# A decoder layer on one core: low parts moved up in a written order of instructions, and one half sum made by a transfer

## The chip, the cores and the metric

The kernel runs on one core of a Trainium2 chip. The metric is the device time of one launch in microseconds (us). TensorE is PE in the profile, with PEld for its weight loads; VectorE is DVE, ScalarE is ACT, GpSimd is POOL, and SyncE is SP, which issues most of the plain transfers. Accumulating transfers (the target becomes target plus source) are issued by POOL.

## What is computed

One decoder layer on x (512 x 1024, float32). Its second half, where the change lies, is

```python
h = layer_norm(ALPHA * h + mixed @ w_out[l], ln1_g[l], ln1_b[l])
a, u = jnp.split(h @ w_ffn_in[l], 2, axis=-1)      # 1024 -> 2 x 2816
a = causal_dwconv(a, conv_w[l], conv_b[l])
f = (jax.nn.gelu(a, approximate=False) * u) @ w_ffn_out[l]
h = layer_norm(ALPHA * h + f, ln2_g[l], ln2_b[l])
```

The first half (projection, block-sparse attention, mean-pool branch, gates, `w_out`) is not touched.

## The kernel before

**Precision.** Every float32 operand of a large product is cut into a high part, written by ACT as float32r, and a low part, written by DVE as source minus high. PE forms high x high, low x high and high x low, so one block of a product is three matmuls.

**The input product of the channel mixer.** The 2816 columns of a and of u are taken in 22 pairs f of 128 columns each. A pair is a 2 x 2 block product and is done with seven block products instead of eight. Its weight tiles are called A (the raw tile of a), X (128 x 1024, two halves, each a sum of a tile half of u and one of a, made by a plain load and an accumulating load on top of it), D (128 x 512) and Y (128 x 1024, made in the place where A lay). Y's first half is A's first half plus X's second half; Y's second half is A's second half plus Y's first half, so it must come later. The operands on the side of h are h itself (hT) and four sums of its blocks, T3, nT2, T4 and nT1, each with a high and a low part.

**The names of the words.** The block products of pair f are A (24 matmuls), and X0, Y0, D, X1 and Y1 (12 matmuls each). X0 uses T3, Y0 uses nT2, D uses T4 and X1 uses nT1. A 0 or 1 after X or Y says which half of the tile, a number behind an underscore the pair. `fnT13` forms nT1 for the last 128 rows of h (row block 3), `hnT13` writes its high part and `lnT13` its low part; `Thi3` and `Tlo3` write the high and the low part of h itself for row block 3. `hX1` and `lX1` write the high and the low part of the weight tile X of pair 1; `y10` and `y11` make the first and the second half of Y of pair 1 on DVE; `cx`, `cy`, `u1`, `u2` and `s` copy and add partial products between PE's groups.

**What sets the order.** For the end of the first layer norm and the first five pairs, the order on PE, ACT and DVE is written by hand, as one list of words (`line`) of which each calls one step. Each engine runs its own steps in the order of that list. The accumulating transfers on POOL follow a second list, `loads(...)`, called at its place in the program; in it "Y1" stands for one half sum of Y of pair 1, made by an accumulating transfer on chip, and "m3" for a one-element write that holds back the load into that home.

```python
def add_y(key):
    raw = raws[key, "A"]
    n = half_sums.get(key, 0)
    c, o = ((slice(0, S), raws[key, "X"][:, S:]), (slice(S, D), raw[:, :S]))[n]
    POOL.dma_start(raw[:, c], o, accum_op=ALU.add)
    half_sums[key] = n + 1

def form_y(key, c):
    raw = raws[key, "A"]
    o = raw[:, :S] if c else raws[key, "X"][:, S:]
    VEC.tensor_tensor(raw[:, c * S:(c + 1) * S], o, raw[:, c * S:(c + 1) * S], op=ALU.add)
    half_sums[key] = c + 1
```

In the trace nearly all of these instructions carry line 67, the line of the recording helper, so they are told apart by their tiles: `sb<-T_..` is X0 or D of a pair, `saf<-nT_..` is Y0 or X1, `saf<-hT_..` is A or Y1. Both tiles called `own` are homes of A and Y: the first for pair 0, the second for pair 1. X of pairs 1 to 4 lies in `fT`.

Of the kernel before, what the change touches and what calls it, by code (L numbers as in the profile page):

```python
# [73 lines left out]
def layer_kernel(ctx: ExitStack, tc: tile.TileContext, xT, x, w_v, w_c, rel_bias, invcnt, w_group,  # L74
# [124 lines left out]
    def loads(line):  # L199
        POOL.on = True  # L200
        for q, n in line.split():
            key = ("f", int(n))
            if q == "Y":
                add_y(key)
            elif q == "m":
                POOL.memset(x_home(int(n))[:, :1], 0.0)
            else:
                coming[q].remove(key)
                fetch_raw(key, q)
        POOL.on = False  # L210
# [12 lines left out]
    def fetch_raw(key, q):  # L223
        a, u = pair_of[key]
        r = raws[key, q] = homes[key[0], q](key[1])
        if q == "A":
            nc.sync.dma_start(r, a)
        elif q == "D":
            state["D", key] = nc.sync.dma_start(r, u[:, S:])
        elif key in SUMMED:  # L230
            state["plain"] = nc.sync.dma_start(r[:, :S], u[:, :S])
        else:
            v = r.rearrange("p (a c) -> p a c", a=2)
            (pst, pn), (est, _) = u.ap
            state["plain"] = nc.sync.dma_start(
                v, bass.AP(tensor=u.tensor, offset=u.offset, ap=[[pst, pn], [0, 2], [est, S]]))
            state["acc"] = POOL.dma_start(
                v, bass.AP(tensor=a.tensor, offset=a.offset, ap=[[pst, pn], [u.offset + S - a.offset, 2], [est, S]]),
                accum_op=ALU.add)
# [3 lines left out]
# [6 lines that stand above are left out]
# [72 lines left out]
    k1, k2 = slice(0, 4), slice(4, 8)  # L321
# [163 lines left out]
    for kt in range(KT):  # L485
# [3 lines left out]
        last = kt == KT - 1  # L489
# [755 lines left out]
    def x_home(f):  # L1245
        if f in tail or f == 4:
            n = tail[f % 4]
            return fT[:, n:n + 2, :].rearrange("p a c -> p (a c)")
        return xraw[f % 2]
# [4 lines left out]
        return end[0][:, f % 2 * S:(f % 2 + 1) * S]  # L1254

    homes["f", "X"], homes["f", "D"] = x_home, d_home
    loads("X1 m3 D0 X2 m4 D1 D2 X3 D3 X4 D4")

    def first(f):
        n = min(tail.values()) - 1 - f // 2  # L1260
# [92 lines left out]
    for i in (2, 3):  # L1353
        for n in parts:
# [6 lines left out]
              ht3=partial(ln1_T, 3), Traw3=partial(T_raw, 3), Thi3=partial(T_hi, 3), Tlo3=partial(T_lo, 3))  # L1361
# [4 lines left out]
    for f in ahead_:  # L1366
# [17 lines left out]
        })  # L1384
    line = """
        fnT12 fT32 A0 st3 hT32 hnT12 A1 hX0 fnT22 mo lT32 hnT22 inv k0 cl3 A2 hY0 cr3 fT42 rs3 hT42 gl lX0
        ht3 k1 lY0 A3 Traw3 lT42 k2 fnT13 Thi3 lnT22 fT33 A4 lnT12 hT33 fnT23 k3 hD0 lT33 hnT23 fT43 X0_0
        lD0 hT43 lnT23 hX1 lT43 Y0_0 hnT13 y10 cx0 Tlo3 D_0 cy0 lnT13 close last lX1 X1_0 y11 X0_1 s_0 hY1
        u2_0 lY1 Y1_0 cx1 hD1 lD1 Y0_1 hX2 y20 s_2 ga0 D_1 lX2 cy1 u1_0 X1_1 y21 s_3 hY2 s_1 X0_2 u2_1 hD2
        lY2 k4 Y1_1 cx2 u1_1 lD2 Y0_2 hX3 gb0 D_2 cy2 lX3 gg0 y31 X1_2 u1_2 hY3 X0_3 u2_2 ga1 s_4 lY3 hD3  # L1390
        Y1_2 cx3 ge0 lD3 Y0_3 ga2 gb1 hX4 D_3 cy3 lX4 gg1 hY4 X1_3 u1_3 ge1 X0_4 hD4 u2_3 lY4 Y1_3 cx4 lD4
        gb2 Y0_4 hA5 ga3 lA5 D_4 cy4 gg2 gb3 X1_4 ge2 gg3 u2_4 ge3 u1_4
    """.split()
    for word in line:
        do[word]()
# [229 lines left out]
```

## Time and profile before

| | us |
|---|---|
| median of 3 runs | 615.79 (615.68 to 1561.75) |
| the profiled execution, its own time | 615.44 |
| span of the profiled execution | 613.6 |
| PE busy in the span | 606.0 |
| DVE busy | 525.0 |
| ACT busy | 376.5 |
| POOL busy | 140.7 |

The span is what the profiler sees between the first and the last instruction; the execution's own time has 1.84 us more around it. The slices of the page show PE busy in nine tenths or more of every slice but the last.

### The profile page before, as it was taken

The page shows a single profiled execution, that of the slowest core. Times are in us where ns is not written, and L with a number is a line of the kernel's source. Part 1 is how long each engine was busy: PE and PEld are TensorE (multiplying, and loading weights), DVE is VectorE, ACT ScalarE, POOL GpSimd, SP SyncE. Part 2 cuts the span into 40 slices and gives each one's busy share as a digit, 9 for nine tenths or more (in the row PEclk, how much of TensorE's full clock was granted, in tenths as well). Part 3 has the DMA queues.
Part 4 walks back from the last instruction along what each step waited for, and adds up shares of the span by engine and source line. Part 5 has one row for each costly group of instructions (what it writes and reads, how often), then busy time and mean ns, then how long its engine had stood idle before and what let it go on. Part 6 is the DMA issues. An engine that isn't in the chain of part 4 may idle for free.

```text
span 613.6 us, 11150 instructions
## 1 busy us (share of the span) xinstructions
PE 606.0 (99%) x4305; PEld 550.2 (90%) x4305; DVE 525.0 (86%) x807; ACT 376.5 (61%) x580; POOL 140.7 (23%) x161
## 2 busy tenths in 40 slices
PE   9999999999999999999999999999999999999995
PEld 6899998767899998888999999999999998888884
DVE  5978876867878888689999899999999998999985
ACT  6536667657556567337666666666666677655861
POOL 0033207360512101211230110102122132532010
PEclk9999999999999999999999999999999999999998
DMA  8767645147776325955999778686998779999324
GB/s 315 224 189 202 174 135 175 36 120 260 202 189 182 79 84 192 330 134 114 279 176 242 187 188 211 186 204 166 223 251 213 198 166 261 306 206 193 61 48 90
DMA packets 45780, 113.39 MB, mean 185 GB/s; under 512 B 4624, under 2 KB 6552, under 8 KB 45728
## 3 DMA queue, kind: packets, MB, share of 16 engines
q0 software_dynamic: 17856, 42.62, 37.1%
q1 hardware_dynamic: 27440, 69.41, 32.8%
q8 instruction: 34, 0.56, 0.3%
q10 hardware_dynamic: 432, 0.66, 0.3%
q14 instruction: 18, 0.15, 0.1%
HBM read 107.80 MB, written 3.69 MB: 182 GB/s over the span
## 4 chain that ended last, share of the span: by engine, by line
PE 99%; DVE 1%; issue 0%
PE saf L67 25%; PE sbf L67 8%; PE br L67 7%; PE wo L67 7%; PE sag L67 6%; PE foa L67 5%; PE fod L67 5%; PE sai L67 5%; PE sbg L67 3%; PE foe L67 3%; PE v L502 3%; PE fob L67 2%; PE sbi L67 2%; PE sb L67 2%; PE g L67 2%; PE p L67 2%
## 5 line engine op out<-in xcount | busy, mean ns | idle before, releaser
L67 ACT ACTIVATE whi<-araw 128x1024 fp32r<-128x1024 f32 x64 | 67.4, 1059 | 29.7 <-PE saf L67 12.5
L67 DVE TENSOR_TENSOR wlo<-araw,whi 128x1024 fp32r<-128x1024 f32 x62 | 75.9, 1242 | 7.6 <-ACT whi L67 5.7
L67 PE MATMUL saf<-hT_hi,wlo 128*128 128x256 f32 x264 | 73.5, 279 | 0.0
L67 PE MATMUL saf<-hT_hi,whi 128*128 128x256 f32 x264 | 73.5, 278 | 0.0
L67 PE MATMUL saf<-hT_lo,whi 128*128 128x256 f32 x264 | 73.2, 277 | 0.0
L67 POOL DMA_DIRECT2D xraw<-in_w_fi x17 | 20.4, 1201 | 132.3 <-DMA xraw<-in_w_fi 80.8
L67 PEld LDWEIGHTS saf<-hT_hi,whi 128*128 128x128 f32 x264 | 49.6, 188 | 0.1
L67 PEld LDWEIGHTS saf<-hT_lo,whi 128*128 128x128 f32 x264 | 49.5, 188 | 0.1
L67 PEld LDWEIGHTS saf<-hT_hi,wlo 128*128 128x128 f32 x264 | 49.6, 188 | 0.0
L67 PE MATMUL saf<-nT_lo,whi 128*128 128x256 f32 x176 | 49.0, 279 | 0.0
L67 PE MATMUL saf<-nT_hi,whi 128*128 128x256 f32 x176 | 49.0, 279 | 0.0
L67 PE MATMUL saf<-nT_hi,wlo 128*128 128x256 f32 x176 | 48.9, 278 | 0.0
L67 DVE TENSOR_TENSOR wlo<-wraw,whi 128x1024 fp32r<-128x1024 f32 (+1 forms) x31 | 36.3, 1181 | 8.7 <-ACT whi L67 8.5
L67 ACT ACTIVATE whi<-wraw 128x1024 fp32r<-128x1024 f32 (+1 forms) x31 | 31.1, 1013 | 14.9 <-DMA wraw<-in_w_v 4.0
L67 ACT ACTIVATE whi<-xraw 128x1024 fp32r<-128x1024 f32 x25 | 26.5, 1063 | 19.8 <-PE saf L67 12.3
L67 PE MATMUL sbf<-T_hi,whi 128*128 128x256 f32 x136 | 37.8, 278 | 0.0
L67 PE MATMUL sbf<-T_hi,wlo 128*128 128x256 f32 x136 | 37.8, 278 | 0.0
L67 PE MATMUL sbf<-T_lo,whi 128*128 128x256 f32 x136 | 37.7, 277 | 0.0
L67 PEld LDWEIGHTS saf<-nT_lo,whi 128*128 128x128 f32 x176 | 33.0, 188 | 0.3 <-DVE nT_lo L67 0.3
L67 PEld LDWEIGHTS saf<-nT_hi,whi 128*128 128x128 f32 x176 | 33.0, 188 | 0.0
L67 PEld LDWEIGHTS saf<-nT_hi,wlo 128*128 128x128 f32 x176 | 33.0, 188 | 0.0
L67 DVE SCALAR_TENSOR_TENSOR y<-saf,cvp,y 128x511 f32<-128x511 f32 (+1 forms) x44 | 32.7, 744 | 0.1
(455 smaller groups left out, 2099.0 us busy)
## 6 DMA issues: line engine op xcount, KB each, us to landing
araw<-in_w_fi SPq DMA_DIRECT2D x20, 512.0 KB, 4.1
xraw<-in_w_fi SPq DMA_DIRECT2D x17, 512.0 KB, 5.3
xraw<-in_w_fi POOLq DMA_DIRECT2D x17, 512.0 KB, 7.5
araw<-in_w_c SPq DMA_DIRECT2D x12, 512.0 KB, 5.0
tw<-in_w_fo POOLq DMA_DIRECT2D x9, 512.0 KB, 7.8
draw<-in_w_fi SPq DMA_DIRECT2D x17, 256.0 KB, 4.3
wraw<-in_w_br SPq DMA_DIRECT2D x8, 512.0 KB, 4.2
wraw<-in_w_out SPq DMA_DIRECT2D x8, 512.0 KB, 3.8
```

The costliest lines, as they stand in the source:

```text
L67: ins = call(*a, **kw)
L502: ins = nc.tensor.matmul(bs[j], xs_[j][a], (wh, wl)[b], start=kt == 0 and n == 0, stop=False)
```

## The change

Five words of the written order change their place, two words trade places, one word goes, and one word is added to the list of transfers:

- `hnT13` (ACT) goes from behind `Y0_0` to before `A4`.
- `lnT23` (DVE), the low part of nT2, comes ahead of `lD0`, the low part of pair 0's D tile.
- `lnT13` (DVE), the low part of nT1, comes ahead of `Tlo3`, the low part of h; the calls `close` and `last` (release of a pool, later transfers) go with it.
- `y10` (DVE) goes. The same sum is made by an accumulating transfer, "Y1" in the list of transfers behind "D2".
- `s_0` and `u2_0` (both DVE) trade places.
- `hY4` and `hD4` (ACT) trade places with words of other engines, which leaves the order on each engine as it is.

```diff
-    loads("X1 m3 D0 X2 m4 D1 D2 X3 D3 X4 D4")
+    loads("X1 m3 D0 X2 m4 D1 D2 Y1 X3 D3 X4 D4")
...
-        ht3 k1 lY0 A3 Traw3 lT42 k2 fnT13 Thi3 lnT22 fT33 A4 lnT12 hT33 fnT23 k3 hD0 lT33 hnT23 fT43 X0_0
-        lD0 hT43 lnT23 hX1 lT43 Y0_0 hnT13 y10 cx0 Tlo3 D_0 cy0 lnT13 close last lX1 X1_0 y11 X0_1 s_0 hY1
-        u2_0 lY1 Y1_0 cx1 hD1 lD1 Y0_1 hX2 y20 s_2 ga0 D_1 lX2 cy1 u1_0 X1_1 y21 s_3 hY2 s_1 X0_2 u2_1 hD2
...
+        ht3 k1 lY0 A3 Traw3 lT42 k2 fnT13 Thi3 lnT22 fT33 hnT13 A4 lnT12 hT33 fnT23 k3 hD0 lT33 hnT23 fT43
+        X0_0 lnT23 hT43 lD0 hX1 lT43 Y0_0 cx0 lnT13 close last Tlo3 D_0 cy0 lX1 X1_0 y11 X0_1 u2_0 hY1 s_0
+        lY1 Y1_0 cx1 hD1 lD1 Y0_1 hX2 y20 s_2 ga0 D_1 lX2 cy1 u1_0 X1_1 y21 s_3 hY2 s_1 X0_2 u2_1 hD2 lY2 k4
```

On DVE, from the low part of T3 to the low part of pair 1's Y tile (`own<-fT,own` is `y10`, `own<-own` is `y11`, `saf<-fT,saf` is `s_0`, `fT<-fT,saf` is `u2_0`), it stood so before:

```order
L67 TENSOR_TENSOR wlo_3504<-fT,whi_3503 128x512
L67 TENSOR_TENSOR nT_lo<-hraw,nT_hi 128x4x128
L67 TENSOR_TENSOR T_lo<-hraw,T_hi 128x4x128
L67 TENSOR_TENSOR own_2889<-fT,own_2889 128x512
L67 TENSOR_TENSOR hT_lo<-ht_0_3420,hT_hi 128x8x64
L67 TENSOR_TENSOR hT_lo<-ht_1_3421,hT_hi 128x8x64
L67 TENSOR_TENSOR nT_lo<-hraw,nT_hi 128x4x128
L67 TENSOR_TENSOR wlo_3526<-fT,whi_3525 128x1024
L67 TENSOR_TENSOR own_2889<-own_2889 128x512
L67 TENSOR_TENSOR saf_3313<-fT,saf_3313 128x256
L67 TENSOR_TENSOR fT<-fT,saf_3313 128x256
L67 TENSOR_TENSOR wlo_3606<-own_2889,whi_3605 128x1024
```

The same place on DVE stands so now:

```order
L67 TENSOR_TENSOR nT_lo<-hraw,nT_hi 128x4x128
L67 TENSOR_TENSOR wlo_3506<-fT,whi_3505 128x512
L67 TENSOR_TENSOR T_lo<-hraw,T_hi 128x4x128
L67 TENSOR_TENSOR nT_lo<-hraw,nT_hi 128x4x128
L67 TENSOR_TENSOR hT_lo<-ht_0_3421,hT_hi 128x8x64
L67 TENSOR_TENSOR hT_lo<-ht_1_3422,hT_hi 128x8x64
L67 TENSOR_TENSOR wlo_3528<-fT,whi_3527 128x1024
L67 TENSOR_TENSOR own_2889<-own_2889 128x512
L67 TENSOR_TENSOR fT<-fT,saf_3314 128x256
L67 TENSOR_TENSOR saf_3314<-fT,saf_3314 128x256
L67 TENSOR_TENSOR wlo_3606<-own_2889,whi_3605 128x1024
```

Both low parts of the h sums have moved one place or three places up, `y10` is gone, and `y11` (`own<-own`) is one place nearer.

On POOL, where the transfers for X of pairs 1 to 4 (`fT<-in_w_fi`) are issued, it stood so before:

```order
L67 DMA fT<-in_w_fi 128x2x512
L67 MEMSET fT 128x1
L67 DMA fT<-in_w_fi 128x2x512
L67 MEMSET fT 128x1
L67 DMA fT<-in_w_fi 128x2x512 x2
L67 DMA araw_3048<-fT 128x512
```

The same place on POOL stands so now:

```order
L67 DMA fT<-in_w_fi 128x2x512
L67 MEMSET fT 128x1
L67 DMA fT<-in_w_fi 128x2x512
L67 MEMSET fT 128x1
L67 DMA own_2889<-fT 128x512
L67 DMA fT<-in_w_fi 128x2x512 x2
L67 DMA araw_3048<-fT 128x512
```

The new half sum (`own<-fT`) is issued behind X's accumulating loads of pairs 1 and 2 and ahead of those of pairs 3 and 4.

## Rows read from the trace of the kernel before

**Rows 1.** The page, part 1: PE's busy time and share of the span.

```profile
PE 606.0 (99%) x4305; PEld 550.2 (90%) x4305; DVE 525.0 (86%) x807; ACT 376.5 (61%) x580; POOL 140.7 (23%) x161
```

**Rows 2.** PEld's waits over the span: us in total, times, longest.

```profile
PEld saf L67 <- DVE nT_lo L67: 0.3, 2, 0.2
...
PEld foa L67 <- ACT whi L67: 0.4, 1, 0.4
```

**Rows 3.** The chain, 293 to 335 us: start, length, what.

```profile
301.56 1.63 PE saf L67 x12
303.19 1.39 PE sb L67 x12
304.57 1.61 PE saf L67 x12
...
307.57 2.77 PE saf L67 x24
```

**Rows 4.** DVE in order of time, 278 to 345 us: start, length, what.

```profile
300.29 0.69 DVE L67 TENSOR_TENSOR wlo<-fT,whi 128x512 fp32r<-128x512 f32 x1
300.89 0.69 DVE L67 TENSOR_TENSOR nT_lo<-hraw,nT_hi 128x512 fp32r<-128x512 f32 x1
...
302.10 0.69 DVE L67 TENSOR_TENSOR own<-fT,own 128x512 f32<-128x512 f32 x1
...
303.90 0.69 DVE L67 TENSOR_TENSOR nT_lo<-hraw,nT_hi 128x512 fp32r<-128x512 f32 x1
...
305.63 0.69 DVE L67 TENSOR_TENSOR own<-own 128x512 f32<-128x512 f32 x1
...
307.45 1.23 DVE L67 TENSOR_TENSOR wlo<-own,whi 128x1024 fp32r<-128x1024 f32 x1 [0.26 <-ACT whi L67]
```

**Rows 5.** ACT in order of time, 278 to 345 us.

```profile
298.06 0.63 ACT L67 ACTIVATE T_hi<-hraw 128x512 fp32r<-128x512 f32 x1 [1.27 <-DVE hraw L67]
...
306.36 1.06 ACT L67 ACTIVATE whi<-own 128x1024 fp32r<-128x1024 f32 x1 [2.75 <-DVE own L67]
```

**Rows 6.** POOL in order of time, 270 to 365 us: its issues of transfers.

```profile
291.19 1.20 POOL L67 DMA_DIRECT2D fT<-in_w_fi  x1 [4.42 <-DMA fT<-in_w_fi]
...
297.05 1.19 POOL L67 DMA_DIRECT2D fT<-in_w_fi  x1 [4.55 <-DMA fT<-in_w_fi]
...
...
307.35 1.20 POOL L67 DMA_DIRECT2D fT<-in_w_fi  x1 [1.09 <-DMA fT<-in_w_fi]
311.74 0.89 POOL L67 DMA_DIRECT2D araw<-fT  x1 [3.19 <-DMA fT<-in_w_fi]
```

**Rows 7.** DMA issues, 291 to 291.5 us: KB, us from issue to landing.

```profile
fT<-in_w_fi POOLq DMA_DIRECT2D x1, 512.0 KB, 9.2
```

**Rows 8.** DMA issues, 297 to 297.2 us.

```profile
fT<-in_w_fi POOLq DMA_DIRECT2D x1, 512.0 KB, 8.9
```

**Rows 9.** DMA issues, 307.3 to 307.6 us.

```profile
fT<-in_w_fi POOLq DMA_DIRECT2D x1, 512.0 KB, 6.9
```

**Rows 10.** DMA issues, 311.7 to 311.8 us.

```profile
araw<-fT POOLq DMA_DIRECT2D x1, 256.0 KB, 3.9
```

**Rows 11.** DMA issues over the span: the on-chip half sums of pairs 0 and 4.

```profile
own<-y POOLq DMA_DIRECT2D x1, 256.0 KB, 3.3
...
araw<-araw POOLq DMA_DIRECT2D x1, 256.0 KB, 6.3
```

**Rows 12.** DMA queues, 301 to 305 us: packets, MB, share of 16 engines.

```profile
q0 software_dynamic: 253, 0.50, 66.9%
```

**Rows 13.** DMA queues, 305 to 307 us.

```profile
q1 hardware_dynamic: 185, 0.33, 48.8%
q0 software_dynamic: 15, 0.02, 6.5%
```

**Rows 14.** Busy time by stretch (PE, PEld, DVE, ACT, POOL), then PE's clock, DMA.

```profile
606.00:608.00 2.00, 0.20 (x1) 0.00 (x0) 1.86 (x8) 0.62 (x2) 0.46 (x1) 1.00 0.65 61
...
609.00:610.00 1.00, 0.00 (x0) 0.00 (x0) 0.96 (x3) 0.24 (x1) 0.00 (x0) 0.50 1.13 225
```

More of the change, by code (lines that the diff above doesn't have):

```diff
@@ L1386, in layer_kernel @@
         fnT12 fT32 A0 st3 hT32 hnT12 A1 hX0 fnT22 mo lT32 hnT22 inv k0 cl3 A2 hY0 cr3 fT42 rs3 hT42 gl lX0
-        ht3 k1 lY0 A3 Traw3 lT42 k2 fnT13 Thi3 lnT22 fT33 A4 lnT12 hT33 fnT23 k3 hD0 lT33 hnT23 fT43 X0_0
-        lD0 hT43 lnT23 hX1 lT43 Y0_0 hnT13 y10 cx0 Tlo3 D_0 cy0 lnT13 close last lX1 X1_0 y11 X0_1 s_0 hY1
-        u2_0 lY1 Y1_0 cx1 hD1 lD1 Y0_1 hX2 y20 s_2 ga0 D_1 lX2 cy1 u1_0 X1_1 y21 s_3 hY2 s_1 X0_2 u2_1 hD2
-        lY2 k4 Y1_1 cx2 u1_1 lD2 Y0_2 hX3 gb0 D_2 cy2 lX3 gg0 y31 X1_2 u1_2 hY3 X0_3 u2_2 ga1 s_4 lY3 hD3
-        Y1_2 cx3 ge0 lD3 Y0_3 ga2 gb1 hX4 D_3 cy3 lX4 gg1 hY4 X1_3 u1_3 ge1 X0_4 hD4 u2_3 lY4 Y1_3 cx4 lD4
-        gb2 Y0_4 hA5 ga3 lA5 D_4 cy4 gg2 gb3 X1_4 ge2 gg3 u2_4 ge3 u1_4
+        ht3 k1 lY0 A3 Traw3 lT42 k2 fnT13 Thi3 lnT22 fT33 hnT13 A4 lnT12 hT33 fnT23 k3 hD0 lT33 hnT23 fT43
+        X0_0 lnT23 hT43 lD0 hX1 lT43 Y0_0 cx0 lnT13 close last Tlo3 D_0 cy0 lX1 X1_0 y11 X0_1 u2_0 hY1 s_0
+        lY1 Y1_0 cx1 hD1 lD1 Y0_1 hX2 y20 s_2 ga0 D_1 lX2 cy1 u1_0 X1_1 y21 s_3 hY2 s_1 X0_2 u2_1 hD2 lY2 k4
+        Y1_1 cx2 u1_1 lD2 Y0_2 hX3 gb0 D_2 cy2 lX3 gg0 y31 X1_2 u1_2 hY3 X0_3 u2_2 ga1 s_4 lY3 hD3 Y1_2 cx3
+        ge0 lD3 Y0_3 ga2 gb1 hX4 D_3 cy3 lX4 gg1 X1_3 u1_3 hY4 ge1 X0_4 u2_3 hD4 lY4 Y1_3 cx4 lD4 gb2 Y0_4
+        hA5 ga3 lA5 D_4 cy4 gg2 gb3 X1_4 ge2 gg3 u2_4 ge3 u1_4
     """.split()
```

## The prediction

> **What bounds the kernel.** I read the page first: PE is busy for 606.0 of 613.6 us [rows 1], so an edit moves the time only where PE waits, or where it makes PE wait. The list of PEld's waits over the span is next. Of the many entries only one names a step that this change moves: the low part of an nT sum, twice, 0.3 us together [rows 2]. The chain in order of time gives the price. A group of 12 matmuls takes 1.39 us. The two groups that hold these waits, `Y0_0` at 301.56 and `X1_0` at 304.57, take 1.63 and 1.61 us [rows 3], so they lose 0.24 and 0.22 us, together 0.46. This is a little more than the waits themselves, and it is all that the moved words can win.
>
> **Who is late.** DVE in order of time answers that. `lnT23` ends at 300.89 + 0.69 = 301.58, just as `Y0_0` begins; `lnT13` ends at 303.90 + 0.69 = 304.59, just as `X1_0` begins [rows 3, 4]. Ahead of them stand `lD0` (300.29), `y10` (302.10) and the low part of h. DVE's starts in this stretch lie 0.60 us apart for such instructions (300.29, 300.89), though each is listed with 0.69 [rows 4].
>
> **The moved words, part by part.** `lnT23` takes `lD0`'s place and ends at 300.29 + 0.69 = 300.98; its high part stood ahead of it before as well. PE's group wants it 0.6 us later, so the 0.24 us go. `lD0` then ends at 301.58; the group that reads it, `D_0`, starts at 303.19 - 0.24 = 302.95, so this costs nothing, with 1.4 us of cover. `lnT13` takes `y10`'s place and ends at 302.10 + 0.69 = 302.79; `X1_0` starts at 304.57 - 0.24 = 304.33, so the 0.22 us go. This needs `hnT13` earlier on ACT, where it now stands before the instruction that sat idle for 1.27 us until 298.06 [rows 5]. Such an instruction takes 0.63 us, so it fits; without that idle time it would push the high part of T3 by 0.63 us. The low part of h keeps its place in time: one instruction of DVE comes ahead of it where another goes. `u2_0` and `s_0` trade places between PE's groups and cost nothing by themselves. Sum of the moves: -0.46 us.
>
> **The half sum as a transfer.** `y10` took 0.60 us of DVE's queue, so DVE reaches `y11` at 305.63 - 0.60 = 305.03. But `y11` reads what the transfer writes, and now waits for it to land. When is that? The transfer reads X of pair 1, whose accumulating load was issued at 291.19 and landed 9.2 us later, at 300.39 [rows 6, 7]. So it is not issued before 300.4. It goes behind the load for X of pair 2, issued at 297.05 and landed 8.9 us later, at 305.95 [rows 6, 8]. The trace of before has no transfer in this place, so I bound its landing:
> - From below, as if nothing stood ahead of it: the half sums of pair 0 took 3.3 us from issue to landing [rows 11], which gives 303.7. That of pair 4, in a busier stretch, took 6.3 [rows 11], which gives 306.7.
> - As POOL's queue behaves further on: X of pair 4 was issued at 307.35 and landed at 314.25; the half sum of pair 3, issued at 311.74 while that load was on its way, landed at 315.64, 1.39 us behind it [rows 6, 9, 10]. The same here gives 305.95 + 1.39 = 307.34.
> - From above, at the pace of the stretch itself: 512 KB took POOL's queue 305.95 - 300.39 = 5.56 us, so 256 KB take 2.78, which gives 308.73.
>
> I take 307.34. The queues decide that for me: between 301 and 305 us POOL's queue, q0, moved 0.50 MB, just the 512 KB of pair 2's load, which had been issued at 297.05 and so lay still until pair 1's had landed [rows 8, 12]. From 305 to 307 q0 moved almost nothing [rows 13]. So the new 256 KB find their place in that gap and not ahead of it.
>
> [...]
>
> **What stands behind the wait.** On DVE `y11`, `u2_0`, `s_0` and `lY1` are queued in this order, and ACT's `hY1` needs `y11`. Before, `lY1` ended at 307.45 + 1.23 = 308.68, which is 3.05 us after `y11` began; ACT's `hY1`, 1.06 us, is the middle of that path [rows 4, 5]. With the transfer at 307.34 the path ends at 310.39. Who wants it: PE's `Y0_1`. The 2.77 us from 307.57 are `Y1_0` and `Y0_1` [rows 3], so `Y0_1` began at 308.96, and with the 0.46 us won it would begin at 308.50. Its third matmul reads the low part, two twelfths of a group (0.23 us) later, at 308.73. So PE waits 310.39 - 308.73 = 1.66 us. Part of that is met one group earlier: `Y1_0` may not begin until `u2_0` has read its bank, and `u2_0` stands behind `y11`; the two waits lie in one another and are not added. For the restarts and the step from a landing to the waiting engine I add 0.2 us, an estimate from rows 2 and 3, where two waits of 0.3 us together cost 0.46. Sum: +1.86 us.
>
> **Does it come back later?** PE stays the bound from here to the end, so a lag of PE is kept. The one later wait in the list, for a high part of an output weight (0.4 us), is priced as it was [rows 2]. X of pairs 3 and 4 queues behind the new 256 KB, which lie in the gap of q0 up to 307, so I cost that at nothing; without the gap their landing moves by 1.4 us, on tiles that PE reads later than all of the above.
>
> **Net and the time.** -0.46 + 1.86 = +1.40 us on the profiled execution's 615.44, so 616.84. The median of the runs lies 0.35 us above that execution (615.79), so the forecast is **617.2 us**. Worked from the bounds of the landing: the loss is zero up to about 305.5 and grows by 1 us for each us beyond; 305.9 is the break-even against the 0.46 won. At 306.7 the net is +0.8 (616.6), at 308.73 it is +2.8 (618.6).
>
> **Rival 1: the transfer lands in time, the kernel is faster.** If the transfer is moved beside pair 2's load instead of behind it, it lands between 303.7 and 305.5, `y11` finds its data and only the 0.46 us won remain: 615.79 - 0.46 = 615.3. For it: the 3.3 us of pair 0's half sums, and the half sum of pair 3 took only 3.9 us from its issue although a load was on its way [rows 10, 11]. Against: pair 2's load itself lay still for 3 us in this very stretch. It decides for this rival if the landing is before 305.5.
>
> **Rival 2: the two waits are won, and the transfer is only a little late.** A landing between 305.5 and 306.7 gives a net between -0.46 and +0.8, so 615.3 to 616.6. The 6.3 us of pair 4's half sum are the row for its upper end.
>
> **Rival 3: PE's wait drops its clock, the kernel is slower by more.** [...] Against it: the forecast wait is in two pieces with a full group between them, and is shorter than the one in rows 14.
>
> **Rival 4: the waits are not won.** Another low or high part could be late in place of the nT sums, for which `hnT13` on ACT and `lD0` are the candidates. Both have cover (0.6 and 1.4 us), so I give it little. With the transfer in time it makes 615.8, no change.
>
> **How the numbers follow.** Chances: forecast (landing beyond 306.7) 0.60, rival 1 0.21, rival 2 0.12, rival 3 0.03, rival 4 0.04. The likeliest gives 617.2, with 616.6 to 618.6 as its own range. The range for 8 in 10 has to reach down to rival 1, so it runs from 615.2 to 618.4, which leaves out rival 3 and the last part of the upper bound. All but the far end of rival 3 lie within 2% (12.3 us), about what a measurement of this kernel can tell from no change: within 2% 0.98, slower 0.01, faster 0.01.
>
> **What the profile of the changed kernel would show.** The groups at 301.56 and 304.3 take 1.39 us each, and the nT entry is gone from PEld's waits: this shows the moves right. DVE sits idle for about 2.3 us before `own<-own`, put down to the transfer `own<-fT`, which takes nearly 7 us from issue to landing; PE waits for DVE near 307 and again near 310; and q0 is busy between 305 and 307 us. If instead `own<-fT` lands within 5 us of its issue and DVE doesn't idle, rival 1 holds. The prediction would be wrong by its queueing step, then, and by nothing else of weight.

## The result and the profile after

The changed kernel takes **619.49 us** (median of 6 runs, 617.47 to 620.64) against 615.73 of the kernel before on the same chip: a ratio of 1.006, 95% interval 1.0041 to 1.0079. That is 3.76 us slower, where the forecast was 1.40 us slower and its range ended at 618.4. The profiled execution of the changed kernel took 620.32 us, with a span of 618.6 us.

The page, part 1, of the changed kernel: PE's busy time and share.

```profile
PE 607.6 (98%) x4305; PEld 551.8 (89%) x4305; DVE 524.5 (85%) x806; ACT 376.3 (61%) x580; POOL 141.8 (23%) x162
```

As many matmuls as in [rows 1], 1.6 us more busy, in a span that is 5.0 us longer. So most of the loss is PE idle, and a part of it is PE busy for longer with the same work.

PE's and PEld's waits in the changed kernel over its span: us in total, times, longest.

```profile
PE saf L67 <- DVE saf L67: 2.3, 1, 2.3
...
PE foa L67 <- ACT whi L67: 0.6, 1, 0.6
...
PEld saf L67 <- DVE saf L67: 2.5, 1, 2.5
```

The entry for nT_lo of [rows 2] is gone, so the two waits that the moved words aimed at are won. A wait of 2.3 us has come in their place. (The longer wait for an output weight, `foa`, belongs to this one execution: another execution of the same kernel, below, doesn't have it.)

PE of the changed kernel in order of time: the first matmuls of `Y0_0`, `D_0`, `X1_0` and `X0_1`, and the last one before the wait.

```profile
301.78 0.28 PE L67 MATMUL saf<-nT_hi,whi 128*128 128x256 f32 x1
...
303.17 0.28 PE L67 MATMUL sb<-T_hi,whi 128*128 128x256 f32 x1
...
304.55 0.28 PE L67 MATMUL saf<-nT_hi,whi 128*128 128x256 f32 x1
...
305.94 0.28 PE L67 MATMUL sb<-T_hi,whi 128*128 128x256 f32 x1
...
307.21 0.28 PE L67 MATMUL sb<-T_hi,wlo 128*128 128x256 f32 x1
```

`Y0_0` and `X1_0` now take 303.17 - 301.78 = 1.39 and 305.94 - 304.55 = 1.39 us.

The chain of the changed kernel from 301 us on, which now leads from transfers through DVE to PE: start, length, what.

```profile
301.24 6.98 DMA own<-fT
...
308.25 0.04 DVE own L67
308.29 0.57 issue
308.86 0.42 DVE fT L67
...
309.31 0.44 DVE saf L67
...
309.79 4.48 PE saf L67 x24
314.27 1.39 PE sb L67 x12
```

In [rows 3] the same stretch was PE alone. Read it downwards: the half sum is issued at 301.24, when X of pair 1 has landed, it lands 6.98 us later, DVE does `y11`, `u2_0` and `s_0` (0.04 + 0.57, 0.42, 0.44 us), and only then does `Y1_0` begin. The row of 24 matmuls is the second loss: `Y1_0` and `Y0_1` together took 2.77 us in [rows 3] and take 4.48 here.

DVE of the changed kernel in order of time, to be held against [rows 4].

```profile
300.67 0.69 DVE L67 TENSOR_TENSOR nT_lo<-hraw,nT_hi 128x512 fp32r<-128x512 f32 x1
...
302.48 0.69 DVE L67 TENSOR_TENSOR nT_lo<-hraw,nT_hi 128x512 fp32r<-128x512 f32 x1
...
308.25 0.69 DVE L67 TENSOR_TENSOR own<-own 128x512 f32<-128x512 f32 x1 [2.75 <-DMA own<-fT]
```

Both nT low parts are earlier, as forecast, and DVE idles for 2.75 us before `y11` and is released by the transfer.

POOL of the changed kernel in order of time: its issues, to be held against [rows 6].

```profile
297.32 1.19 POOL L67 DMA_DIRECT2D fT<-in_w_fi  x1 [4.36 <-DMA fT<-in_w_fi]
...
301.24 0.89 POOL L67 DMA_DIRECT2D own<-fT  x1 [2.62 <-DMA fT<-in_w_fi]
```

DMA issues of the changed kernel, 297.2 to 297.5 us: KB, us to landing.

```profile
fT<-in_w_fi POOLq DMA_DIRECT2D x1, 512.0 KB, 9.0
```

DMA queues of the changed kernel, 305 to 307 us: packets, MB, share.

```profile
q0 software_dynamic: 154, 0.28, 76.1%
```

Pair 2's load lands at 297.32 + 9.0 = 306.32, just as late after its issue as in [rows 8], and the half sum at 301.24 + 6.98 = 308.22, 1.9 us behind it. POOL's queue, almost idle between 305 and 307 us in [rows 13], is now filled there.

The stretches of the changed kernel: busy time of PE, PEld, DVE, ACT and POOL, then PE's granted clock, the DMA share and GB/s.

```profile
307.00:308.00 1.00, 0.49 (x5) 0.29 (x3) 0.00 (x0) 0.00 (x0) 0.00 (x0) 1.00 0.90 227
308.00:309.00 1.00, 0.00 (x0) 0.00 (x0) 0.75 (x2) 0.03 (x1) 0.07 (x1) 1.00 0.96 178
309.00:310.00 1.00, 0.21 (x1) 0.21 (x2) 0.70 (x2) 1.00 (x2) 1.00 (x1) 0.74 1.10 205
310.00:311.00 1.00, 1.00 (x5) 1.00 (x6) 0.94 (x1) 1.00 (x4) 0.13 (x1) 0.50 1.14 148
311.00:312.00 1.00, 1.00 (x7) 1.00 (x6) 1.00 (x3) 0.77 (x1) 0.00 (x0) 0.50 0.48 78
312.00:313.00 1.00, 1.00 (x7) 1.00 (x6) 1.00 (x3) 0.24 (x1) 0.28 (x1) 0.55 1.09 201
313.00:314.00 1.00, 1.00 (x11) 1.00 (x11) 1.00 (x2) 0.54 (x1) 0.72 (x2) 1.00 1.10 203
```

Here is the rest of the loss. PE stops in the second half of 307 us and is idle until 309.79; the granted clock falls from 1.00 to 0.50 and stays there until shortly before 313 (0.50 from 312.50 to 312.75, 0.72 on average from 312.75 to 313.00). It fell before PE was at work again: from 309 to 310 us PE worked only the last 0.21 us, and the mean clock of that microsecond is already down to 0.74; from 309.40 to 309.60 it is 0.69, from 309.60 to 309.79 it is 0.50, both with PE idle. In the three microseconds from 310 to 313 PE is listed as fully busy and yet issues 5 to 7 matmuls per microsecond instead of 11.

### The profile page after: what moved, and what is told of

Its sections match the earlier page's. It is cut to its first block, busy times and chain, and to the rows that moved or that the text cites. A ratio compares the mean times of both kernels' runs of the same rounds, so it can differ in the third digit from the quotient of the medians.

```text
span 618.6 us, 11153 instructions
## 1 busy us (share of the span) xinstructions
PE 607.6 (98%) x4305; PEld 551.8 (89%) x4305; DVE 524.5 (85%) x806; ACT 376.3 (61%) x580; POOL 141.8 (23%) x162
## 4 chain that ended last, share of the span: by engine, by line
PE 93%; DMA 5%; DVE 1%; issue 0%; ACT 0%; SPq 0%; ACTq 0%
PE saf L67 22%; PE sbf L67 8%; PE br L67 7%; PE wo L67 7%; PE sag L67 6%; PE fod L67 5%; PE sai L67 5%; PE foa L67 4%; PE sbg L67 3%; PE foe L67 3%; PE v L502 3%; PE fob L67 2%; DMA fT<-in_w_fi 2%; PE sbi L67 2%; PE g L67 2%; PE p L67 2%
```

## The experiments

Diffs are against the changed kernel, unless said otherwise. The theory is: the moves win 0.46 us; the transfer queues behind pair 2's load and holds up `Y1_0`; the idle PE then loses its clock.

**The two halves of the change apart.** In moves_only the half sum is back on DVE.

```diff
-    loads("X1 m3 D0 X2 m4 D1 D2 Y1 X3 D3 X4 D4")
+    loads("X1 m3 D0 X2 m4 D1 D2 X3 D3 X4 D4")
-  ... Y0_0 cx0 lnT13 close last Tlo3 ...
+  ... Y0_0 cx0 lnT13 y10 close last Tlo3 ...
```

> The changed order, but the first half of pair 1's Y sum is again made by VectorE, behind nT1's low part, and the transfer is gone. Theory (the whole loss is the wait for the transfer and what follows from it; the moved low parts win 0.46 us): 0.46 us under the kernel before, about 615.3, with the two groups of Y0_0 and X1_0 at 1.39 us each. Rival (the moves themselves, or the swap of the two small steps behind them, cost something): at or above 615.8, or above it by 1 us and more.

Measured: 615.48 against 615.33 us, ratio 0.9998 (0.9989 to 1.0007), no change. The interval reaches as far down as 0.46 us, so the time alone can't tell this gain from none. The chain of moves_only, start, length, what, shows where most of it went:

```profile
302.03 1.39 PE saf L67 x12
303.41 1.39 PE sb L67 x12
304.80 1.39 PE saf L67 x12
306.19 1.50 PE sb L67 x12
307.69 3.01 PE saf L67 x24
```

`Y0_0` and `X1_0` are down to 1.39 us, but the groups behind them grew by 0.11 and 0.24 us, so 0.35 of the 0.46 us is given back. With `y10` behind `lnT13`, DVE hands over `y11` and what follows later. The moves alone shift the lateness from one step to the next; it takes one instruction less on DVE for them to pay, as sum_on_gpsimd shows below.

In transfer_only the order is that of before, without `y10` and with the transfer (diff against the kernel before).

```diff
-    loads("X1 m3 D0 X2 m4 D1 D2 X3 D3 X4 D4")
+    loads("X1 m3 D0 X2 m4 D1 D2 Y1 X3 D3 X4 D4")
-  ... Y0_0 hnT13 y10 cx0 Tlo3 ...
+  ... Y0_0 hnT13 cx0 Tlo3 ...
```

> The order before, with the one VectorE sum replaced by the transfer, at the same place in the list of transfers as in the change. Theory: the transfer lands at the same time, so PE stalls as in the changed kernel and its clock falls; the 0.46 us are not won, and freeing 0.6 us on VectorE wins nothing: 619 to 620.5. Rival (the loss needs the swapped steps or the earlier release of the pool): below 617.

Measured: 617.85 against 615.33 us, ratio 1.0042 (1.0028 to 1.0056). PE's wait in transfer_only and, after it, two stretches of that kernel:

```profile
PE saf L67 <- DVE fT L67: 2.2, 1, 2.2
```

```profile
309.00:310.00 1.00, 0.35 (x3) 0.35 (x4) 0.64 (x3) 1.00 (x3) 0.92 (x1) 1.00 1.15 213
310.00:311.00 1.00, 1.00 (x11) 1.00 (x10) 1.00 (x2) 1.00 (x3) 0.00 (x0) 1.00 0.72 100
```

The transfer alone makes the wait and, without any of the moves, a slowdown of 2.5 us. This is less than the 619 to 620.5 us expected, since the clock held at 1.00 in this profile. By the mean granted clock of each execution (0.997 to 0.998 in four, 0.994 in one, which took 619.57 us against 617.27 to 617.96) it held in four of five.

**Is it the order in the queue?** Two kernels move the transfer in POOL's list: ahead of pair 2's load, and behind pair 3's.

```diff
-    loads("X1 m3 D0 X2 m4 D1 D2 Y1 X3 D3 X4 D4")
+    loads("X1 m3 D0 Y1 X2 m4 D1 D2 X3 D3 X4 D4")    transfer_first
+    loads("X1 m3 D0 X2 m4 D1 D2 X3 Y1 D3 X4 D4")    transfer_later
```

> The changed kernel, with the half sum issued ahead of the accumulating load for X of pair 2 instead of behind it. Theory (the transfer is late because it queues behind that load): it lands 3.3 to 5 us after its issue at about 301, so between 304.3 and 306, PE waits for at most 1 us and the clock holds: 615.3 to 616.5. Pair 2's load, issued some 4 us later than before, lands near 309 and is read at about 308.4, so up to 1 us of wait may come in its place. Rival (the transfer is slow by itself in this busy stretch, in whatever place): it takes near 7 us again and the time stays at 619 or more.

Measured: 617.92 against 615.33 us, ratio 1.0046 (1.0033 to 1.0059). The DMA issue of transfer_first, KB and us to landing:

```profile
own<-fT POOLq DMA_DIRECT2D x1, 256.0 KB, 3.4
```

With nothing ahead of it the transfer lands 3.4 us after its issue, not 7.0: what it waits for in the changed kernel is pair 2's load. The time is lost elsewhere, since POOL issues pair 2's load only at 301.92 us and it lands at 310.12. PE then waits 0.6 us until 312.20 for a copy by ACT, which stands on ACT behind the high part of that late tile, and further on 0.8 us until 331.93 for a low part of DVE and 0.4 us until 335.60 for another copy by ACT. The clock stays at 1.00. So the change of place moved the loss from one tile to later ones.

> The changed kernel with the half sum issued one place later still, behind the accumulating load for X of pair 3. Theory (the transfer lands behind whatever load stands ahead of it in POOL's queue): that load landed at 311.5 to 312.5 in every run so far, so the half sum lands at about 313 to 314, some 5 us later than in the changed kernel; PE's wait grows to 7 us or more, the clock falls in every execution, and the time is 623 to 626. Rival (the landing is set by the busy stretch before 307 and not by the load ahead): it lands near 309, as in the changed kernel, and the time stays at 619 to 621.

Measured: 624.36 against 615.18 us, ratio 1.0144 (1.0131 to 1.0158), so 9.2 us slower. The chain of transfer_later and, after it, its stretches:

```profile
306.18 6.43 DMA own<-fT
...
314.17 5.49 PE saf L67 x24
```

```profile
312.00:313.00 1.00, 0.00 (x0) 0.00 (x0) 0.37 (x1) 0.00 (x0) 0.93 (x2) 0.89 1.10 201
313.00:314.00 1.00, 0.00 (x0) 0.00 (x0) 0.97 (x3) 0.64 (x1) 0.00 (x0) 0.50 1.13 209
```

One place further back in the queue, the landing moves to 312.61 and PE's wait grows to 6.7 us. The clock is again down before PE starts, and it stays down under all 24 matmuls (0.50 from 314 to 315, 0.54 on average from 315 to 320), which take 5.49 us instead of 2.77. The stall of 6.7 and the 2.7 us of clock, less 0.46, make 8.9 of the 9.2 us.

**Is it the clock?** If PE is given other work while it waits, the wait shrinks and the clock should hold. One, two or three groups of 12 matmuls are put ahead of `Y1_0`; their product is used by nothing.

```diff
+    do["fill"] = lambda: s_mm(("f", 1), "X", 0, tt["T3"], low_(2), True)
-        lY1 Y1_0 cx1 ...
+        lY1 fill Y1_0 cx1 ...               one_group
+        lY1 fill fill Y1_0 cx1 ...          filled_wait
+        lY1 fill fill fill Y1_0 cx1 ...     three_groups
```

> The changed kernel with two extra groups of 12 matmuls (a repeat of pair 1's X0 group, into the bank that pair 2 overwrites later) put where PE waits; 2.77 us of added PE work whose result isn't used. Theory (the wait costs twice, once as a stall of about 2.4 us and once as the lower clock behind it, about 1.6 us): the stall is filled, the clock stays at 1.00, and the kernel with the added work is faster than the changed one, by about 1.5 us: 618.0. Rival (the slow matmuls behind the wait come from something else, such as the transfers): they stay slow, and the time is that of the changed kernel or up to 0.4 us more.

Measured: 618.20 against 615.33 us, ratio 1.0043 (1.0031 to 1.0056). The chain of filled_wait:

```profile
301.45 8.32 DMA own<-fT
...
311.33 3.05 PE saf L67 x24
```

The clock held in every execution (mean 0.996 to 0.998) and the 24 matmuls take 3.05 us. PE still waits 0.9 us, as the transfer landed later here (8.3 us from its issue). With 2.77 us of useless work added, the median lies below that of the changed kernel, though their intervals overlap.

> The changed kernel with one extra group of 12 matmuls (1.39 us of PE work whose result isn't used) where PE waits. Theory: 1 us of the wait is left, the clock holds, and the time is that of an execution of the changed kernel whose clock held, about 617.4 to 618. Rival (any wait of this place lowers the clock): 619 and more.

Measured: 619.07 against 615.55 us, ratio 1.0051 (1.0036 to 1.0066). Two stretches of one_group:

```profile
311.00:312.00 1.00, 1.00 (x10) 1.00 (x10) 1.00 (x1) 1.00 (x3) 0.00 (x0) 0.92 0.89 152
312.00:313.00 1.00, 1.00 (x7) 1.00 (x6) 1.00 (x3) 0.94 (x2) 0.62 (x2) 0.50 1.12 207
```

The transfer landed 8.3 us after its issue here as well, so that the wait was 2.3 us as before, in spite of the added group, and the clock fell, here only when PE had been at work again since 310.71. By the mean clock it fell in two of the six executions (0.995, 619.73 and 619.99 us) and held in four (0.997 to 0.998), of which three took 618.53 to 619.18 us all the same. The run does not separate the theories: it changed the work and, by chance or not, the landing with it.

> The changed kernel with three extra groups of 12 matmuls (4.16 us of PE work whose result isn't used) where PE waits. Theory: they cover the wait even where the transfer lands 8.3 us after its issue, so no wait and no lower clock is left: the kernel before, minus 0.46, plus 4.16, so 3.7 us above it, in every execution, with a mean clock of 0.996 or more; the changed kernel, which has none of this work, takes 3.8 to 4.3 us more than the kernel before. Rival (other costs of the transfer remain): 5 us and more above the kernel before.

Measured: 618.83 against 615.18 us, ratio 1.006 (1.0047 to 1.0073), 3.65 us more. The chain of three_groups, where one row holds `X0_1` and the three added groups:

```profile
305.69 5.55 PE sb L67 x48
311.24 2.77 PE saf L67 x24
```

No wait is left, the clock stays at 1.00, and the 24 matmuls take 2.77 us again. The added work, 3 x 1.39 = 4.16 us, less the 0.46 won, is 3.70 us: as expected. The changed kernel, which has none of that work, is as slow. So its stall and its clock together cost about as much as 36 matmuls, and no further cost of the transfer shows.

**The changed kernel once more,** unaltered, since its six runs spread over 3 us.

> The changed kernel itself, beside the next three on one chip. Theory (a stall of about 2.4 us, and in most executions a lower clock behind it for 1.6 us): two kinds of executions, near 617.4 with a mean granted clock of 0.997 or more and near 619.4 with 0.995 or less, more of the second kind. Rival (the spread is in the transfer's landing and not in the clock): the times spread evenly and don't go with the clock.

Measured: 619.88 against 615.55 us, ratio 1.0069 (1.0052 to 1.0086). The profiled execution was by chance the fastest, 617.72 us. Its stretches and, after them, its chain:

```profile
309.00:310.00 1.00, 0.57 (x4) 0.57 (x5) 0.67 (x2) 1.00 (x3) 0.77 (x1) 1.00 1.10 203
310.00:311.00 1.00, 1.00 (x11) 1.00 (x10) 1.00 (x2) 1.00 (x2) 0.00 (x0) 1.00 1.03 98
```

```profile
309.43 3.06 PE saf L67 x24
```

The same program, the same wait (2.4 us), a held clock: 3.06 us for the 24 matmuls against 4.48, and no wait for `foa`. This is the cleanest price of the clock, 4.48 - 3.06 = **1.42 us**. The other five executions, with a mean clock of 0.992 to 0.995, took 619.55 to 621.65 us. In the first series it was alike: 617.47 us at a mean clock of 0.997, the other five 619.22 to 620.64 at 0.993 to 0.995. In these ten the fall is read from the mean clock (0.996 and more in every execution of the kernel before) and the time; only two executions have a trace, one that lost its clock and one that kept it. The transfer landed 7.0 and 7.1 us after its issue in these two and up to 8.5 in other runs, so a later landing may have added to the time of some of the ten.

**Can the wait be covered by order alone?** In y11_behind `u2_0` and `s_0` go ahead of the waiting `y11`, so that `Y1_0` isn't blocked by them.

```diff
-  ... X1_0 y11 X0_1 u2_0 hY1 s_0 lY1 Y1_0 cx1 ...
+  ... X1_0 X0_1 u2_0 s_0 y11 Y1_0 hY1 lY1 cx1 ...
```

> The changed kernel with the waiting VectorE step (the second half of pair 1's Y sum) put behind the two small steps that PE's next group needs. Theory: the transfer lands as before, PE goes on for one group more and then waits in two pieces, for the high and the low part of that tile, about 2.2 us in all; no wait is as long as the 2.3 us in the changed kernel, so the clock holds in every execution: about 617.3, some 2 us under the changed kernel. Rival (the length of PE's wait in one piece doesn't matter for the clock): as the changed kernel, 619 and more.

Measured: 620.36 against 615.55 us, ratio 1.008 (1.0068 to 1.0092). It was expected to do better and didn't. `Y1_0` does run without a wait. PE then stops one group later, 2.7 us for ACT's high part and 0.7 us for DVE's low part, as the transfer landed 8.5 us after its issue, and the clock is down to 0.50 by 314 us. By the mean clock it fell in three of the five executions (0.993); the two others (0.996) took as long, 620.17 and 620.36 us, so here the clock doesn't tell the times apart. `Y0_1` needs the sum itself, and no order on DVE changes when that lands.

**The same sum without a queue.** In sum_on_gpsimd the changed order stays, and GpSimd makes the half sum by an instruction at the place where it issued the transfer. gpsimd_only is transfer_only with the same edit.

```diff
-    POOL.dma_start(raw[:, c], o, accum_op=ALU.add)
+    if key == ("f", 1):
+        POOL.tensor_tensor(raw[:, c], o, raw[:, c], op=ALU.add)
+    else:
+        POOL.dma_start(raw[:, c], o, accum_op=ALU.add)
```

> The changed order, with the first half of pair 1's Y sum made by a GpSimd instruction at the place where the transfer stood in its queue. Theory (the moved low parts win 0.46 us if VectorE is freed of 0.6 us and nothing waits for the queue of transfers): the sum takes about 1.7 us, as the GpSimd sums of the same size earlier in the kernel, starts when X of pair 1 has landed, near 301, and ends near 303, two us before it is read; 0.3 to 0.5 us faster than the kernel before. Rival (GpSimd is slower beside a busy VectorE, or slows it): no gain, or a wait of PE as in the changed kernel.

Measured: 614.50 against 615.55 us, ratio 0.9986 (0.9978 to 0.9994). POOL and, after it, the chain in sum_on_gpsimd:

```profile
301.28 3.18 POOL L67 TENSOR_TENSOR own<-fT,own 128x512 f32<-128x512 f32 x1 [2.63 <-DMA fT<-in_w_fi]
```

```profile
302.10 1.39 PE saf L67 x12
...
304.87 1.39 PE saf L67 x12
...
307.64 2.77 PE saf L67 x24
```

The sum is there at 301.28 + 3.18 = 304.46, before DVE reaches `y11`, every group takes its 1.39 us, and PE doesn't wait between 290 and 330 us. The instruction is longer than the 1.7 us expected (one GpSimd sum of that shape took 1.68 us, at 240.40 in the kernel before); POOL had nothing else to do.

> The order before, with the one VectorE sum made by a GpSimd instruction, at the place in GpSimd's queue where the change had the transfer. Theory: VectorE is 0.6 us ahead from that place on, so the wait of X1_0 (0.22 us) goes and that of Y0_0 (0.24 us) stays: 0.2 us under the kernel before, about half of what the changed order with the same GpSimd sum won. Rival (the GpSimd sum alone makes the gain, or none of it): as far under the kernel before as with the changed order, or not under it.

Measured: 615.26 against 615.18 us, ratio 0.9995 (0.9986 to 1.0004), not to be told from no change. The chain of gpsimd_only:

```profile
301.43 1.63 PE saf L67 x12
```

`Y0_0` still takes 1.63 us there, as in [rows 3], so the moves are needed for its 0.24 us.

> The changed order with the half sum as a GpSimd instruction, a second time on another occasion, since its first result (ratio 0.9986, 0.9978 to 0.9994) lies close to no change. Theory: the two waits that the moved words win (0.46 us) are won and nothing is lost, so about 0.5 us below the kernel before (ratio 0.9993), and the first result's 1.05 us were in part scatter. Rival: the gain of about 1 us is real, ratio near 0.9985, and something beyond the two waits is won. Third: no gain, ratio 1.000. In the profile every group of 12 between 300 and 315 us takes 1.39 us and the clock stays at 1.00.

Measured: 615.39 against 615.52 us, ratio 0.9997 (0.9988 to 1.0006), with every group at 1.39 us again. So of the two series one is just below the kernel before and one is level with it. The profile shows both waits won, 0.46 us. The times fit that, and don't measure it: 1.05 us in the first series is more than the trace accounts for, 0.13 in the second is less. As the better way to write this change it is clear of the scatter: 4 to 5 us below the changed kernel.

## Why the prediction was off

**Right.** The moved words win 0.46 us: the two groups went from 1.63 and 1.61 [rows 3] to 1.39 us, and `Y1_0` would have begun 0.46 us earlier on a common clock (PE's first matmul of `X0_0` starts 0.38 us later in the profile after). That they win only if DVE is relieved as well was not said; moves_only shows it. The direction, the place, DVE's idle time before `y11`, the 7 us of the transfer and the filled q0 came as forecast, and transfer_first and transfer_later show the step from the queue's order. Rivals 1 and 2, an early landing, fall, and so does rival 4, since the two waits are won.

**Off in size: the stall.** Three sums, of the profile after:
- Landing. Forecast 1.39 us behind pair 2's load, from the half sum of pair 3 [rows 9, 10]; measured 308.22 - 306.32 = 1.90. That is 0.5 us more.
- The path behind it. The forecast followed the long way over `lY1` to `Y0_1` and said that the wait comes in two pieces. It came in one, at `Y1_0`: `s_0` had been put behind `u2_0`, both stand behind `y11`, and from the landing to PE's start it is 309.79 - 308.22 = 1.57 us. The long path ends later, but PE has all of `Y1_0` to do before it needs it; the short one ends first, and PE has nothing to do until then. So the short one decides. PE's last matmul before it started at 307.21, so `Y1_0` was due 0.12 us later, at 307.33, and lost 2.46 us.
- Restart: in changed_again, at full clock, the first 0.12 us go there.

Together 2.58 us where the forecast had 1.86.

**The step that failed: that the clock holds.** The forecast has no term for the clock and leaves its fall to rival 3, which was given a chance of 0.03, because the wait would be "in two pieces with a full group between them, and is shorter than the one in rows 14". The first half of that was wrong, as shown. The second was no argument: in the stretch of [rows 14] one wait of 1.9 us (606.20 to 608.12) ended at clock 1.00, and the clock was down about one microsecond later (0.81 on average from 608.80 to 609.00, 0.50 from there on); that doesn't show a wait that is safe. In ten of twelve executions of the changed kernel the clock fell, for 1.42 us. This takes the time out of the stated range: the larger stall alone leaves it inside, as the two executions that kept the clock show (617.47 and 617.72 us against an end at 618.4).

The sum as measured: -0.46 + 2.58 + 1.42 = **+3.54 us**, beside 3.76 between the medians. Without the fall it is +2.12, and the executions that kept the clock, 617.47 and 617.72 us, are 1.74 and 2.17 above the medians of before: the forecast of 617.2 us was for these, and they are the rarer ones.

Whether another execution holds or loses its clock after the same wait is not settled by any run here.

## What to carry over

A transfer that takes an instruction off a busy engine is paid at its landing, not at its issue: count what stands ahead of it on its own queue, and price it with its place in that queue (3.4 us from issue to landing alone, 7.0 to 8.5 behind one load, and 6.7 us of wait on PE with the issue one place further back). A stall of PE near 2 us costs its own length and may cost the clock after it (PE waits of 2.2 to 2.4 us here, followed by clock 0.50 in two profiles of four), so a forecast should carry that term with a real chance; one profile can show either case, so look at several executions' clocks. If the engine that issues the transfer is idle anyway, let it compute the small sum itself (here 4 to 5 us less than with the transfer).

## What the runs showed of the hardware

- **The clock after equal waits.** PE waits of 2.2 to 2.4 us were followed by clock 0.50 in two profiles (the changed kernel, one_group) and by 1.00 in two others (transfer_only, changed_again). The clock then stayed at 0.50 for about 3 us of PE's work. In the changed kernel and in transfer_later, with 6.7 us of wait, it was down before the wait had ended; in one_group PE had been at work again for about 1 us.
- **Two landings of one transfer.** In the same place in the queue the half sum took 7.0 to 7.1 us in four profiles (the changed kernel, changed_again, transfer_only, three_groups) and 8.3 to 8.5 in three (filled_wait, one_group, y11_behind). PE at work is not the reason, since three_groups has PE busy throughout and the short time. The cause stays open.
- **A GpSimd sum that stretches.** The half sum of 128 x 512 took 3.18 and 3.22 us in the changed order and 2.36 us in gpsimd_only, while five two-input instructions of that shape, in another part of the kernel, take 1.29 us on average, so the half sum took 1.8 to 2.5 times as long as those. (Three more GpSimd sums of that shape took 1.30, 1.68 and 6.80 us in the kernel before.) A busy DVE alone is not the difference: DVE was busy for 1.53 of the 1.60 us around one of the five (202.00 to 203.60 in the kernel before). But beside each of these five a DVE low part of 128 x 512 was listed with 1.52 to 1.58 us instead of 0.69, while beside the half sum DVE's instructions of that shape stayed at 0.68 to 0.69. So in one place DVE's instruction is the longer one and in the other GpSimd's; why was not tried.
